# Input-projection features: the context's high and low parts in one 512-column matmul, runs of equal width, and the rotary key's high and low weights in one stationary tile

## Chip, cores and metric

The kernel runs on one core of a Trainium2 chip. The metric is the device time of one launch in microseconds (us). The core has a matrix engine (TensorE, PE in the profile; PEld is its loading of stationary tiles), a vector engine (VectorE, DVE), a scalar engine (ScalarE, ACT), GpSimd (POOL) and SyncE (SP), which here does nothing but issue DMA transfers, one after the other in program order.

## What is computed

One layer of a transformer over 512 latent tokens and 256 context tokens, width 2048, batch 1. The part that matters here is the combined input projection and the modulation that goes beside it:

```python
def _mixer_inputs(h, tabs, w_in, q_norm_w, kv_norm_w, w_uq, w_ukv):
    p = h @ w_in
    q_da = heads(p[..., :o1], DA_HEADS)
    k_da = heads(p[..., o1:o2], DA_HEADS)
    v_da = heads(p[..., o2:o3], DA_HEADS)
    c_q = _rmsnorm(p[..., o3:o4], q_norm_w)
    c_kv = _rmsnorm(p[..., o4:o5], kv_norm_w)
    k_rope = p[..., o5:][:, None]
```

`h` is the normalised and modulated input. The projection is made for the latent tokens and for the context tokens with the same weights; keys, values and the compressed key/value latent `c_kv` are wanted for both, queries and the compressed query latent `c_q` for the latent tokens alone. `k_rope`, the rotary key that all heads share, has 64 features. The keys of the latent tokens are rotated (rotary embedding). Beside it stands the conditioning, a matrix-vector product (GEMV) `silu(c) @ w_ada` of 96 blocks of 128 outputs, whose results modulate later stages. Everything is float32 to within a narrow tolerance.

## The kernel before

**Three matmuls for one product.** TensorE multiplies tiles in a reduced float32 form (`F32R`). To keep the accuracy, every operand is split into a high part (the rounded value) and a low part (what rounding left), and `mm3` makes a product out of three matmuls: high by high (L258), high by low (L259), low by high (L260). The weights arrive as blocks of 128 x 1024 float32: `wblock` (L241) has SP load the block into `wr` (L244), ACT round it into `wh` (L234), and DVE subtract to give `wl` (L235). There are three buffers each of `wr`, `wh`, `wl`.

**Stages.** Up to about 46 us a prologue normalises the input and starts the conditioning. Up to about 155 us "group 0" makes the first features of the projection beside the preparation of the 16 k-tiles of `h` (function `features(kt)`, laid out by a planner with due times, `Flow(PLAN)`). It leaves in SBUF, for each k-tile, the latent tokens' high and low parts (`hx[kt]`, two tiles `a2k` of 512 columns) and the context tokens' (`hc[kt]`, high and low, 256 columns each). Before the change, two k-tiles share a pair of `c2k` tiles: the high parts of both lie in one and the low parts of both in the other.

From about 155 to 446 us runs the part that the change is in. It is written as plain code, and the framework's scheduler sets the order of each engine's instructions; tiles are drawn from rings, and who draws a tile waits until its last reader is done.

- Seven context features, `f` = 0 to 6 in the loop: six are keys of the differential attention (`k_d[2]` to `k_d[7]`), the seventh is the rotary key (`kr_d`). Each has two weight blocks of eight k-tiles. In `feature` (L739) each k-tile makes three matmuls of 512 columns into a PSUM tile `b` (latent) and three of 256 columns into a PSUM tile `s` (context). `keys` (L685) then rotates the latent half on DVE (L304 to L307), splits both halves (L234 on ACT, L235 on DVE) into `kh` and `kl`, and `put` (L694) has SP write those to `k_d` (L696). The rotary key has 64 features; the host has laid its 64 weight columns twice beside each other in the block of 128.
- After each of these features, `next_gemv(kv, 3)` makes three GEMV blocks: SP loads 1 MB into `ada` (L323, two buffers), DVE multiplies it by the conditioning vector and sums (L326), the result is one column of `modx`. The blocks come from one list, and who calls `next_gemv` takes the next of it; the list holds 48.
- Three query-latent features, `feature(lat, None)`: latent tokens only, 48 matmuls of 512 columns each, two GEMV blocks behind each. Then `latent_norm(cq)` normalises them: its sum of squares is made by PE into a PSUM tile `s`, and DVE's `rstd` reads it last at L316 (`n`).
- The value projection, two halves of eight weight blocks, which reads `hx` and `hc` as stationary tiles 128 columns wide. Its first half takes two `s` tiles and two `b` tiles; there are only two `s` tiles, so the second of them is the one that the norm's L316 reads. Behind each weight block stand one or two GEMV blocks, until the list is empty.

Behind it the attention begins, at about 446 us, again laid out by a planner; then the output projection and the feed-forward part, to the end.

SP issues weight loads, `ada` loads and writes of keys in one order. An issue whose buffer isn't free holds up all that stand behind it.

Of the kernel before, what the change touches and what calls it, by code (L numbers as in the profile page):

```python
# [206 lines left out]
def layer_kernel(ctx: ExitStack, tc: tile.TileContext, small, rope, c_row, cc_row, x_t, ctx_t, ada, ada_k,  # L207
# [23 lines left out]
    def split(dst_h, dst_l, src, scale=None):  # L231
# [337 lines left out]
    def features(kt):  # L569
# [13 lines left out]
        for i, (src, cut, c, hl, g) in enumerate(((at_x[kt], slice(0, T), slice(0, T), xh, 1.0),  # L583
                                                  (at_c[kt // 2], o, slice(T, TT), mine, 0.6))):
            b, th = (modx, modc)[i][:, kt:kt + 1], buf(lambda: None)
            out = (slice(0, T), o)[i]
# [3 lines left out]
            step("ACT", 0.63 * g, t - 3.2 + 1.2 * i, lambda h=h, c=c, b=b, hl=hl, out=out: sc.activation(  # L590
                hl[0]()[:, out], h()[:, c], AF.Identity, bias=b), r=[th, at_b[i][kt]], w=[hl[0]])
            step("DVE", 0.67 * g, t - 2.4 + 1.2 * i, lambda h=h, c=c, b=b, hl=hl, out=out: ve.scalar_tensor_tensor(
                out=hl[1]()[:, out], in0=h()[:, c], scalar=b, in1=hl[0]()[:, out].bitcast(F32), op0=ALU.add,
                op1=ALU.subtract), r=[th, hl[0], at_b[i][kt], h], w=[hl[1]])
# [11 lines left out]
        for f in range(4):  # L606
# [4 lines left out]
            step("PE", 0.36, t + 1 + 0.1 * f + (5 if kt == KT - 1 and f > 1 else 0), mm, r=[hi, lo, *mine],  # L611
                 w=[ctx_bufs[f // 2]])

    hc_bufs = []
# [22 lines left out]
    with tc.manual_schedule(engines={mybir.EngineType.PE, mybir.EngineType.Activation, mybir.EngineType.DVE,  # L637
# [10 lines left out]
    wsrc = iter([w_f[f, hf] for f in feats for hf in range(2)] + [w_v[half, kb] for half in range(2) for kb in range(8)]  # L648
                + [w_f[7 + h, hf] for h in range(7) for hf in range(2)])
    wready = []  # L650

    def ahead(count):
        while len(wready) < count:
            src = next(wsrc, None)
            if src is None:
                return
            wready.append(wblock(src))
# [24 lines left out]
    def rtmp():  # L682
        return kv.tile([P, T], F32, tag="rt", name=nm("rt"), bufs=2)

# [1355 lines left out]
```

## Time and profile before

| | before |
|---|---|
| device time, median of 3 runs | 2364.34 us (2362.61 to 2366.74) |
| profiled execution, span from first to last instruction | 2365.8 us |
| mean granted TensorE clock | 0.992 of full speed |
| prologue and group 0, 0 to 155.6 us: PE busy | 129.8 us |
| context and query-latent features, 155.6 to 314 us: PE busy | 154.6 of 158.4 us |
| the same: DVE busy, ACT busy | 128.2 us, 38.0 us |
| the same: DMA | busy share 0.87, 313 GB/s |
| value projection, 314 to 446 us: PE busy | 132.0 of 132.0 us |
| the rest, 446 to 2365 us: PE busy | 1891.4 of 1919 us |

The span is that of one profiled execution; it lies 1.5 us above the median of the timed runs and inside their spread. Rows of the timeline give the start of an instruction in us from the span's start, its duration, engine, line and operation, output and inputs, and in brackets how long the engine stood idle before it and what ended that. Rows of groups give the busy time and the mean duration in ns of the like instructions taken together, and behind the bar the idle time just before them. Rows of waits give who waited for what: us in all, how often, the longest. The rows of the DMA view give KB of a transfer and the median us from its issue to its landing.

### The profile page before, as it was taken

To read this page: it belongs to the slowest core of one execution; us is meant where nothing else is said; L and a number is where in the kernel's file an instruction comes from. 1 tells how busy PE (TensorE), PEld (TensorE's weight loads), DVE (VectorE), ACT (ScalarE), POOL (GpSimd) and SP (SyncE) were. 2 spreads that over 40 slices of the span, in tenths; PEclk is the share of its full clock that TensorE was granted. 3 is DMA by queue.
4 is the path that set the end of the run, shared out by engine and by line. 5 is a ranking of instruction groups with operands and counts; after the bars stand their busy time and mean duration, and the time that the engine had idled before them with its cause. 6 is when DMAs were issued, how large, how long until landed. Compare 5 with 4: busy or idle time off the path is not lost.

```text
span 2365.8 us, 32444 instructions
## 1 busy us (share of the span) xinstructions
PE 2307.7 (98%) x12526; PEld 1969.6 (83%) x12526; DVE 1733.4 (73%) x2248; ACT 1140.3 (48%) x1736; POOL 255.5 (11%) x290
## 2 busy tenths in 40 slices
PE   5999999999999999999999999999999999999998
PEld 3788878888788888898888888888888888888887
DVE  8997776498977766598585858585857576767767
ACT  5331221377866622365454545454545454544546
POOL 0000000100033213000101010101010101011110
PEclk8999999999999999999999999999999999999999
DMA  9968989644411187334737464646465556465573
GB/s 350 341 251 302 324 307 342 189 138 122 146 65 40 46 331 286 103 107 112 166 105 170 113 160 118 152 125 149 127 143 134 143 135 147 119 161 125 142 189 107
DMA packets 130492, 404.25 MB, mean 171 GB/s; under 512 B 14337, under 2 KB 25089, under 8 KB 119841
## 3 DMA queue, kind: packets, MB, share of 16 engines
q1 hardware_dynamic: 103858, 351.64, 44.4%
q0 software_dynamic: 25328, 49.49, 12.0%
q8 instruction: 98, 1.61, 0.3%
q10 hardware_dynamic: 1152, 1.05, 0.1%
q14 instruction: 56, 0.46, 0.1%
HBM read 332.45 MB, written 69.67 MB: 170 GB/s over the span
## 4 chain that ended last, share of the span: by engine, by line
PE 78%; issue 9%; DVE 5%; DMA 5%; ACT 2%; POOL 1%; SPq 0%; DVEq 0%; ACTq 0%; POOLq 0%
PE y L1759 11%; PE b L258 9%; PE b L259 9%; PE b L260 9%; PE z L1759 6%; PE y L1761 5%; PE s L862 4%; PE s L258 4%; PE s L259 3%; PE s L260 3%; DMA ada<-in_ada 3%; PE z L1761 3%; PE x L1759 2%; PE f L258 2%; PE f L259 1%
## 5 line engine op out<-in xcount | busy, mean ns | idle before, releaser
L1584 DVE TENSOR_TENSOR wl<-wr,wh 128x1024 fp32r<-128x1024 f32 x144 | 176.4, 1225 | 155.8 <-ACT wh L1576 155.1
L1780 POOL DMA_DIRECT2D x_d<-xs x160 | 139.7, 1001 | 1158.7 <-ACT xs L1779 1156.3
L1576 ACT CAST wh<-wr 128x1024 fp32r<-128x1024 f32 x144 | 151.0, 1049 | 230.9 <-PE b L259 119.6
L258 PE MATMUL b<-ah,wh 128*128 128x512 f32 (+1 forms) x664 | 256.8, 387 | 0.0
L259 PE MATMUL b<-al,wh 128*128 128x512 f32 (+1 forms) x664 | 256.7, 387 | 0.0
L260 PE MATMUL b<-ah,wl 128*128 128x512 f32 (+1 forms) x664 | 255.8, 385 | 0.0
L1584 DVE TENSOR_TENSOR wl<-rb,wh 128x1024 fp32r<-128x1024 f32 x123 | 150.0, 1219 | 126.9 <-ACT wh L1576 126.9
L1576 ACT CAST wh<-rb 128x1024 fp32r<-128x1024 f32 x123 | 129.3, 1051 | 184.1 <-PE b L259 116.1
L1584 DVE TENSOR_TENSOR wl<-ws,wh 128x1024 fp32r<-128x1024 f32 x123 | 150.1, 1220 | 90.0 <-ACT wh L1576 90.0
L1576 ACT CAST wh<-ws 128x1024 fp32r<-128x1024 f32 x123 | 128.1, 1042 | 131.1 <-DVE ws L1538 45.4
L326 DVE CUSTOM_DVE_ANT_0 ada<-ada,cb,smt 128x2048 f32<-128x2048 f32 x64 | 152.6, 2391 | 43.5 <-DMA ada<-in_ada 43.4
L1759 PE MATMUL y<-a2k,wh 128*128 128x512 f32 x656 | 164.0, 392 | 0.0
L234 ACT CAST wh<-wr 128x1024 fp32r<-128x1024 f32 x53 | 55.7, 1052 | 197.5 <-DMA wr<-in_w_o 48.8
L260 PEld LDWEIGHTS b<-ah,wl 128*128 128x128 f32 x664 | 124.8, 188 | 25.7
L258 PEld LDWEIGHTS b<-ah,wh 128*128 128x128 f32 x664 | 125.1, 188 | 22.9
L259 PEld LDWEIGHTS b<-al,wh 128*128 128x128 f32 x664 | 125.1, 188 | 22.0
L258 PE MATMUL b<-a2k,wh 128*128 128x512 f32 (+1 forms) x372 | 139.2, 374 | 1.9 <-DVE n L1657 1.7
L259 PE MATMUL b<-a2k,wh 128*128 128x512 f32 (+1 forms) x372 | 138.4, 372 | 0.0
L260 PE MATMUL b<-a2k,wl 128*128 128x512 f32 (+1 forms) x372 | 137.7, 370 | 0.3 <-DVE wl L235 0.3
L1759 PEld LDWEIGHTS y<-a2k,wh 128*128 128x128 f32 x656 | 118.6, 189 | 21.6
L867 ACT ACTIVATE p<-s,m 128x768 f32<-128x768 f32 x96 | 86.8, 905 | 42.4 <-DVE m L865 39.2
L1759 PE MATMUL y<-b2k,wh 128*128 128x512 f32 x410 | 106.9, 391 | 0.0
(479 smaller groups left out, 5815.4 us busy)
## 6 DMA issues: line engine op xcount, KB each, us to landing
ada<-in_ada SPq DMA_DIRECT2D x80, 1024.0 KB, 7.0
rb<-in_w_up SPq DMA_DIRECT2D x123, 512.0 KB, 4.4
wr<-in_w_dn SPq DMA_DIRECT2D x88, 512.0 KB, 4.1
x_d<-xs POOLq DMA_DIRECT2D x160, 256.0 KB, 6.0
wr<-in_w_up SPq DMA_DIRECT2D x53, 512.0 KB, 4.2
wr<-in_w_f SPq DMA_DIRECT2D x34, 512.0 KB, 7.8
adak<-in_ada_k SPq DMA_DIRECT2D x32, 512.0 KB, 6.2
wr<-in_w_o SPq DMA_DIRECT2D x32, 512.0 KB, 6.5
```

What stands on the lines that cost most here:

```text
L234: sc.copy(dst_h, src)
L258: pe.matmul(out, st[0], mv[0], start=start, stop=False, **kw)
L259: pe.matmul(out, st[0], mv[1], start=False, stop=False, **kw)
L260: pe.matmul(out, st[1], mv[0], start=False, stop=stop, **kw)
L326: ve.tensor_tensor_reduce(out=junk, in0=w, in1=vec, op0=ALU.mult, op1=ALU.add, scale=1.0, scalar=col("b_ada", j), accum_out=dst[:, j:j + 1])
L862: pe.matmul(s()[:, c0:c1], a, b[:, c0:c1], start=i == 0, stop=i == len(ms) - 1)
L867: step("ACT", 0.9, t + cost + 1.2, lambda: sc.activation(p(), s()[:, :TT], AF.Exp, bias=m(), accum_out=lcol()), r=[s, m], w=[p, l], lag=0.25)
L1576: sc.copy(t, raw[:, k * n_:k * n_ + n_])
L1584: ve.tensor_tensor(t, raw[:, k * n_:k * n_ + n_], hi[k].bitcast(F32), op=ALU.subtract)
L1759: pe.matmul(o, w[j][0], hs[j], start=start and j == 0, stop=False, skip_group_check=True)
L1761: pe.matmul(o[:, h0], w[j][1], hs[j][:, h0], start=False, stop=j == 7, skip_group_check=True)
L1780: gp.dma_start(x1_d[dt], x, accum_op=ALU.add)
```

## The change

**The context's two parts in one matmul.** Each k-tile of the context now has a `c2k` tile of its own with the high part in columns 0 to 255 and the low part in columns 256 to 511 (`hcb[kt]` is the whole tile, `hc[kt]` the two halves). In `feature`, high weights by high context and high weights by low context become one matmul of 512 columns (`wide`) into a PSUM tile of 512 columns; low weights by high context stays a matmul of 256 columns (`narrow`) into its left half. `halves_sum` then adds the two halves: ACT copies the left one to SBUF, DVE adds the right one.

**Runs of equal width.** A weight block's matmuls are no longer ordered k-tile by k-tile but in runs: the first block's 24 latent ones, then 8 wide, then 8 narrow; the second block's 8 narrow, 8 wide, 24 latent.

**The rotary key.** Its block of 128 columns now holds the high parts of the 64 weights in columns 0 to 63 of each k-tile and the low parts in columns 64 to 127 (`rotary_block`). So a k-tile has three matmuls of 512 columns (latent high, latent low, and the context tile with both parts), and the results for high and low weights stand in the upper and lower 64 partitions; `parts_sum` adds each half to the other, so that both hold the sum, as before. The product of the two low parts is now part of the sum.

**One GEMV block** less behind the rotary key (2 instead of 3). The list is the same, so the value projection takes one more.

```diff
+    def rotary_block(src):
+        raw = wp.tile([P, 1024], F32, tag="wr", name=nm("wr"), bufs=3)
+        nc.sync.dma_start(raw, src)
+        w = wp.tile([P, 1024], F32R, tag="wh", name=nm("wh"), bufs=3)
+        sc.copy(w, raw)
+        low, src = (t.rearrange("p (k f) -> p k f", f=P)[:, :, 64:] for t in (w, raw))
+        ve.tensor_tensor(low, src, low.bitcast(F32), op=ALU.subtract)
+        return w, None
...
-        if kt % 2 == 0:
-            hc_bufs.append([buf(lambda: c2k(F32R), "c2k", 17) for _ in range(2)])
-            mine = hc_bufs[-1]
-        else:
-            mine = [buf(lambda b=b: b()) for b in hc_bufs[-1]]
+        mine = buf(lambda: c2k(F32R), "c2k", 17)
...
-                    hc[kt] = tuple(b()[:, o] for b in mine)
+                    hc[kt] = mine()[:, :C], mine()[:, C:]
+                    hcb[kt] = mine()
...
-            wready.append(wblock(src))
+            wready.append(rotary_block(src) if rotary else wblock(src))
...
+    def halves_sum(co):
+        t = kv.tile([P, C], F32, tag="ct", name=nm("ct"), bufs=2)
+        sc.copy(t, co[:, :C])
+        ve.tensor_tensor(t, co[:, C:], t, op=ALU.add)
+        return t
...
-    def feature(lat, ctxo):
+    def feature(lat, co):
         for hf in range(2):
             wh, wl = next_block()
+            ws = [(hf * 8 + j, wh[:, j * P:(j + 1) * P], wl[:, j * P:(j + 1) * P]) for j in range(8)]
+            def latent():
+                for kt, *w in ws:
+                    mm3(lat, w, hx[kt], kt == 0, kt == KT - 1)
+            def wide():
+                for kt, w, _ in ws:
+                    pe.matmul(co, w, hcb[kt], start=kt == 0, stop=False, skip_group_check=True)
+            def narrow():
+                for kt, _, w in ws:
+                    pe.matmul(co[:, :C], w, hc[kt][0], start=False, stop=kt == KT - 1, skip_group_check=True)
+            for part in (latent, wide, narrow)[::-1 if hf else 1] if co is not None else (latent,):
+                part()
+        ahead(2)
+
+    def rotary_feature(lat, co):
+        for hf in range(2):
+            w, _ = next_block()
             for j in range(8):
                 kt = hf * 8 + j
-                w = (wh[:, j * P:(j + 1) * P], wl[:, j * P:(j + 1) * P])
-                mm3(lat, w, hx[kt], kt == 0, kt == KT - 1)
-                if ctxo is not None:
-                    mm3(ctxo, w, hc[kt], kt == 0, kt == KT - 1)
+                for out, mv in ((lat, hx[kt][0]), (lat, hx[kt][1]), (co, hcb[kt])):
+                    pe.matmul(out, w[:, j * P:(j + 1) * P], mv, start=kt == 0 and mv is not hx[kt][1],
+                              stop=kt == KT - 1 and mv is not hx[kt][0])
         ahead(2)
+    def parts_sum(src, t):
+        sc.copy(t[lo], src[hi])
+        sc.copy(t[hi], src[lo])
+        ve.tensor_tensor(t, src, t, op=ALU.add)
+        return t
...
     for f in range(7):
-        lat, co = b_tile(), s_tile()
-        feature(lat, co[:, :C])
-        keys(k_d[f + 2] if f < 6 else kr_d, lat, co[:, :C])
-        next_gemv(kv, 3)
+        lat, co = b_tile(), s_tile()[:, :T]
+        if f < 6:
+            feature(lat, co)
+            keys(k_d[f + 2], lat, halves_sum(co))
+        else:
+            rotary_feature(lat, co)
+            lat = parts_sum(lat, kv.tile([P, T], F32, tag="qs0", name=nm("lt"), bufs=1))
+            keys(kr_d, lat, parts_sum(halves_sum(co), kv.tile([P, C], F32, tag="ct", name=nm("ct"), bufs=2)))
+        next_gemv(kv, 3 if f < 6 else 2)
```

The change moves instructions on four engines; all stands within the features, from about 155 us to the start of the value projection. In the rows below, the line comes first, then the operation, output and inputs with a running number of the tile, and the shape. Lines from L241 on stand 10 further down in the changed kernel, and those from `keys` on 14.

On PE, two k-tiles of a context feature before the change (`b` is the latent result, `s` the context's; `a2k` and `c2k` are the latent and context operands):

```order
L258 MATMUL b_2378<-a2k_442,wh_2345 128x512
L259 MATMUL b_2378<-a2k_455,wh_2345 128x512
L260 MATMUL b_2378<-a2k_442,wl_2346 128x512
L258 MATMUL s_2379<-c2k_449,wh_2345 128x256
L259 MATMUL s_2379<-c2k_450,wh_2345 128x256
L260 MATMUL s_2379<-c2k_449,wl_2346 128x256
L258 MATMUL b_2378<-a2k_538,wh_2345 128x512
L259 MATMUL b_2378<-a2k_566,wh_2345 128x512
L260 MATMUL b_2378<-a2k_538,wl_2346 128x512
L258 MATMUL s_2379<-c2k_568,wh_2345 128x256
L259 MATMUL s_2379<-c2k_579,wh_2345 128x256
L260 MATMUL s_2379<-c2k_568,wl_2346 128x256
```

And after it, where the first block of a context feature passes from its latent run to its wide run and then to its narrow run:

```order
L269 MATMUL b_1580<-a2k_947,wh_1472 128x512
L270 MATMUL b_1580<-a2k_849,wl_1473 128x512
L765 MATMUL s_1581<-c2k_449,wh_1472 128x512
L765 MATMUL s_1581<-c2k_472,wh_1472 128x512
L765 MATMUL s_1581<-c2k_579,wh_1472 128x512
L765 MATMUL s_1581<-c2k_568,wh_1472 128x512
L765 MATMUL s_1581<-c2k_729,wh_1472 128x512
L765 MATMUL s_1581<-c2k_764,wh_1472 128x512
L765 MATMUL s_1581<-c2k_861,wh_1472 128x512
L765 MATMUL s_1581<-c2k_956,wh_1472 128x512
L769 MATMUL s_1581<-c2k_449,wl_1473 128x256
L769 MATMUL s_1581<-c2k_472,wl_1473 128x256
```

A k-tile thus has five matmuls instead of six, and all 256-column ones of a feature stand in one run, across its two blocks. The rotary key has three per k-tile.

On SP, between the sixth key and the rotary key, before (`wr` are weight blocks, `ada` the GEMV's blocks, `kh` and `kl` the key that is written to `k_d`; the two weight blocks are those of the rotary key):

```order
L244 DMA wr_2343<-in_w_f 128x1024
L244 DMA wr_2349<-in_w_f 128x1024
L323 DMA ada_2369<-in_ada 128x2048
L696 DMA k_d_134<-kh_2228 128x768
L696 DMA k_d_134<-kl_2229 128x768
L323 DMA ada_2372<-in_ada 128x2048
L323 DMA ada_2375<-in_ada 128x2048
```

and after:

```order
L244 DMA wr_2262<-in_w_f 128x1024
L244 DMA wr_2267<-in_w_f 128x1024
L710 DMA k_d_134<-kh_2163 128x768
L333 DMA ada_2289<-in_ada 128x2048
L710 DMA k_d_134<-kl_2164 128x768
L333 DMA ada_2292<-in_ada 128x2048
L333 DMA ada_2295<-in_ada 128x2048
```

The write of `kh` has moved ahead of the first `ada` load. At two of the earlier features the third `ada` load has moved ahead of the second weight load.

On DVE, at the query-latent norm, before (`n` is L316, the last reader of the norm's `s` tile; `wl_2846` is the low part of the value projection's third weight block, the L326 rows are the GEMV):

```order
L326 ISA ada_2718,modx<-ada_2718,cb_1488,smt 128x2048
L326 ISA modx 128x1
L326 ISA ada_2721,modx<-ada_2721,cb_1488,smt 128x2048
L326 ISA modx 128x1
L235 TENSOR_TENSOR wl_2846<-wr_2843,wh_2845 128x1024
L316 TENSOR_SCALAR n_2729<-s_2724 128x512
L317 SCALAR_TENSOR_TENSOR n_2730<-nr_2728 128x512
L318 TENSOR_TENSOR n_2730<-n_2730,n_2729 128x512
```

and after:

```order
L336 ISA ada_2598,modx<-ada_2598,cb_1488,smt 128x2048
L336 ISA modx 128x1
L336 ISA ada_2601,modx<-ada_2601,cb_1488,smt 128x2048
L336 ISA modx 128x1
L326 TENSOR_SCALAR n_2609<-s_2604 128x512
L327 SCALAR_TENSOR_TENSOR n_2610<-nr_2608 128x512
L235 TENSOR_TENSOR wl_2726<-wr_2723,wh_2725 128x1024
L328 TENSOR_TENSOR n_2610<-n_2610,n_2609 128x512
```

The third value block's `wl` has moved from ahead of `n` to behind it. On PE, at the start of the value projection, the matmuls into the first `s` tile and the `b` tiles that stand ahead of the first one into the second `s` tile are 15 instead of 7. The orders of group 0, up to about 155 us, are as before on all engines.

More of the change, by code (lines that the diff above doesn't have):

```diff
@@ L609, in mm @@
                 mm3(ctx0(f), w, hc[kt], kt == 0 and f % 2 == 0, kt == KT - 1, skip=True)
-            step("PE", 0.36, t + 1 + 0.1 * f + (5 if kt == KT - 1 and f > 1 else 0), mm, r=[hi, lo, *mine],
+            step("PE", 0.36, t + 1 + 0.1 * f + (5 if kt == KT - 1 and f > 1 else 0), mm, r=[hi, lo, mine],
                  w=[ctx_bufs[f // 2]])
-    hc_bufs = []
+    hcb = [None] * KT
     g0s = [buf(s_tile, "s", 2) for _ in range(2)]
@@ L647, in layer_kernel @@
     feats = list(range(7)) + [14, 15, 16]
-    wsrc = iter([w_f[f, hf] for f in feats for hf in range(2)] + [w_v[half, kb] for half in range(2) for kb in range(8)]
-                + [w_f[7 + h, hf] for h in range(7) for hf in range(2)])
+    wsrc = iter([(w_f[f, hf], f == 6) for f in feats for hf in range(2)] + [(w_v[half, kb], False) for half in range(2) for kb in range(8)]
+                + [(w_f[7 + h, hf], False) for h in range(7) for hf in range(2)])
     wready = []
@@ L653, in ahead @@
         while len(wready) < count:
-            src = next(wsrc, None)
+            src, rotary = next(wsrc, (None, False))
             if src is None:
                 return
-            wready.append(wblock(src))
+            wready.append(rotary_block(src) if rotary else wblock(src))
     def next_block():
```

10 lines of the change are left out of this document (5 added, 5 removed).

## Prediction

> **What bounds the kernel now.** I read the page first, then the 8-us windows, the waits and the timelines of the stretch in which the changed lines run (150 to 320 us).
>
> ```profile
> span 2365.8 us, 32444 instructions
> PE 2307.7 (98%) x12526; PEld 1969.6 (83%) x12526; DVE 1733.4 (73%) x2248; ACT 1140.3 (48%) x1736; POOL 255.5 (11%) x290
> ...
> 286.00:294.00 8.00, 8.00 (x37) 6.64 (x36) 3.84 (x5) 1.05 (x1) 0.00 (x0) 1.00 0.96 372
> ...
> 302.00:310.00 8.00, 8.00 (x31) 5.37 (x29) 4.96 (x7) 2.13 (x3) 0.00 (x0) 1.00 0.84 319
> 310.00:318.00 8.00, 4.16 (x11) 3.17 (x11) 6.22 (x7) 2.26 (x3) 0.00 (x0) 0.68 0.88 327
> 318.00:326.00 8.00, 8.00 (x33) 6.52 (x32) 7.90 (x11) 2.59 (x4) 0.00 (x0) 0.89 0.71 247
> ```
>
> PE is busy 98% of the span. (Columns of a window: length, then busy time and instructions of PE, PEld, DVE, ACT, POOL, then granted clock, DMA share, GB/s.) In the changed stretch PE is full up to 310 us, then loses 3.84 of 8 us while the clock falls to 0.68. Beside it the DMA engines are 0.84 to 0.96 busy: two limits lie close together here. The wait itself, on PE:
>
> ```profile
> 309.74 0.39 PE L258 MATMUL b<-wh,c2k 128*128 128x512 f32 x1
> 313.97 0.80 PE L258 MATMUL s<-wh,a2k 128*128 128x512 f32 x1 [3.84 <-DVE n L316]
> 314.56 0.63 PE L259 MATMUL s<-wl,a2k 128*128 128x512 f32 x1
> ...
> 319.68 0.45 PE L260 MATMUL s<-wh,a2k 128*128 128x512 f32 x1
> ```
>
> This is the start of the value projection: its second `s` tile is the one that the query-latent norm has just used, and DVE's L316 (`n`) is the last to read it. What stood ahead of L316 on DVE:
>
> ```profile
> 307.09 2.35 DVE L326 CUSTOM_DVE_ANT_0 ada<-ada,cb,smt 128x2048 f32<-128x2048 f32 x1 [2.68 <-DMA ada<-in_ada]
> ...
> 309.81 2.35 DVE L326 CUSTOM_DVE_ANT_0 ada<-ada,cb,smt 128x2048 f32<-128x2048 f32 x1 [0.36 <-DMA ada<-in_ada]
> ...
> 312.09 1.22 DVE L235 TENSOR_TENSOR wl<-wr,wh 128x1024 fp32r<-128x1024 f32 x1
> 313.23 0.68 DVE L316 TENSOR_SCALAR n<-s 128x512 f32<-128x512 f32 x1
> ```
>
> So the stretch ends with DVE's queue, which waits for `ada` loads. That chain, over the whole stretch:
>
> ```profile
> L326 DVE CUSTOM_DVE_ANT_0 ada<-ada,cb,smt 128x2048 f32<-128x2048 f32 x27 | 63.4, 2348 | 21.7 <-DMA ada<-in_ada 21.7
> L235 DVE TENSOR_TENSOR wl<-wr,wh 128x1024 fp32r<-128x1024 f32 x23 | 27.9, 1218 | 2.5 <-ACT wh L234 2.4
> ...
> SPq L323 <- DVE modx L326: 75.5, 20, 7.4
> ...
> ada<-in_ada SPq DMA_DIRECT2D x26, 1024.0 KB, 7.8
> ```
>
> There are two `ada` buffers. SP issues a load when DVE has finished the buffer (SP waits 75.5 us for this), it lands after 7.8 us, DVE then takes 2.35: one `ada` per (7.8 + 2.35) / 2 = 5.1 us, whatever PE does. 27 of them stand ahead of L316.
>
> **The change part by part.** *PE work.* The period of a context feature, and matmuls without a context:
>
> ```profile
> 160.47 0.40 PE L258 MATMUL b<-a2k,wh 128*128 128x512 f32 x1
> ...
> 161.28 0.28 PE L259 MATMUL s<-c2k,wh 128*128 128x256 f32 x1
> 161.40 0.28 PE L260 MATMUL s<-c2k,wl 128*128 128x256 f32 x1
> ...
> 173.07 0.40 PE L258 MATMUL b<-a2k,wh 128*128 128x512 f32 x1
> ...
> 301.69 0.39 PE L258 MATMUL b<-a2k,wh 128*128 128x512 f32 x1
> ...
> 305.54 0.40 PE L260 MATMUL b<-a2k,wl 128*128 128x512 f32 x1
> ```
>
> From 160.47 to 173.07 lie 12 groups of three 512- and three 256-column matmuls: 1.05 us each, 16.8 us a feature. From 301.69 to 305.54 lie 17 starts of 512 columns: 0.2265 us each; a 256-column one starts 0.12 us after its like. A new feature has 48 + 16 wide and 16 narrow matmuls: 64 x 0.2265 + 16 x 0.12 = 16.4 us, 0.4 less; six give 2.3 us. The rotary one has 48 wide: 10.9 us, 5.9 less. PE work falls by 8.2 us.
>
> A rule speaks against the first part: the Trainium skill, "TensorE: Matmul & The Clock Gate", section "Part 1: The HAM clock gate", puts warm back-to-back matmuls at N / 2.4 GHz plus 2.5 ns, so one 512-column matmul in place of two of 256 would save 2.5 ns, 0.3 us over the six features (an estimate by that page). The rows differ (0.2265 and 0.12 against its 0.216 and 0.109), and the measurement decides.
>
> *What is late next.* If PE comes 8.2 us sooner to the value projection, it waits for L316 unless L316 comes sooner too. So the sum is that of L316, in four terms:
>
> - One GEMV is moved from ahead of L316 to behind it (7 x 3 + 3 x 2 = 27 become 26): one period, **-5.1**. From the bytes it would be 1.05 MB at the 319 to 372 GB/s of the windows, some 3 us.
> - L316 now stands ahead of the third value block's `wl`, not behind it: 313.23 - 312.09 = **-1.1**.
> - DVE gets seven sums of 256 columns for the context halves, and for the rotary key one of 512 and one of 256; its two low parts are half as wide.
>
> ```profile
> L307 DVE TENSOR_TENSOR rt<-rt,rt 128x512 f32<-128x512 f32 x10 | 6.8, 683 | 0.0
> ...
> L235 DVE TENSOR_TENSOR kl<-s,kh 128x256 fp32r<-128x256 f32 x7 | 2.9, 407 | 0.0
> ```
>
>  8 x 0.41 + 0.68 - 2 x (1.22 - 0.68) = 2.9 us. Bounds: 0, if they fall into the 21.7 us in which DVE waits for `ada`, and 2.9. I take **+2.9**, since in the new order they stand between two `ada` steps of a chain whose buffer is free only afterwards. The strided half-width subtraction has no row; between 0.68 (512 contiguous) and 1.22 (full width) I take 0.68, worth at most 1.1 us.
> - SP's order: the write of a key's `kh` now stands ahead of the next feature's first `ada`; before, it stood behind it. The rows of that place before:
>
> ```profile
> 245.75 0.33 SPq L323 DMA_DIRECT2D ada<-in_ada  x1
> 247.01 0.33 SPq L696 DMA_DIRECT2D k_d<-kh  x1
> 251.47 0.33 SPq L696 DMA_DIRECT2D k_d<-kl  x1
> ```
>
>  The `ada` would have gone out 1.3 us later behind `kh`. Two of the first features also have an `ada` drawn ahead of a weight load, which helps the chain. Bounds 0 and one period (5.1); I take **+2**, nearer to the 1.3 of these rows.
>
> Sum for L316: -5.1 - 1.1 + 2.9 + 2.0 = -1.3. In the new PE order 15 matmuls of the value projection run ahead of the wait, before it 7: 8 x 0.2265 = **-1.8** behind it. Together **-3.1 us**; by the bounds, -8.0 to -0.1.
>
> The first stage (up to 155 us) costs nothing: the order of all engines and the shapes are as before there. ACT's copies (seven of 256 columns, some small ones for the rotary key) hide in its idle time: ACT is 48% busy. Behind the value projection the order is as before, apart from one GEMV more, and PE runs there without a wait; a shift at its start arrives at the end.
>
> *Weights.* DVE makes the first query block's `wl` behind the third `ada` of the feature before:
>
> ```profile
> 264.11 2.34 DVE L326 CUSTOM_DVE_ANT_0 ada<-ada,cb,smt 128x2048 f32<-128x2048 f32 x1
> ...
> 266.98 1.22 DVE L235 TENSOR_TENSOR wl<-wr,wh 128x1024 fp32r<-128x1024 f32 x1
> ```
>
> It is ready at 268.2; PE needed it at 272.9 and will at 264.7, so PE waits some 3 us there, and again at the next blocks. It costs nothing as long as these waits sum to less than PE would wait for L316 anyway: 8.2 + 3.84 - 1.3 - 1.8 = 8.9 us of cover.
>
> The sum is made on the profiled span (2365.8), which lies 1.5 us above the median of the runs (2364.34) and inside their spread; I take the difference from the median: 2364.34 - 3.1 = **2361.2 us**.
>
> **The rivals.** *The waits are spread.* If the 8.9 us of waiting fall apart into pieces at the three query features and at the value projection, each shorter than the 3.84 of now, the clock may not fall: 14 matmuls from 313.97 to 319.68 took 0.41 instead of 0.2265 us, 2.5 us in all. Then -3.1 - 2.5 = -5.6: 2358.7. For it: the new `wl` waits lie in between. Against: one of them may be as long as today's. The rule that fits (the Trainium skill, same page and section): the clock halves after an idle window of about 3.4 us, and the trace agrees, with 3.84 us idle ahead of the 0.68.
>
> *PE alone sets the end.* If the DMAs land sooner, since PE no longer competes with anything of theirs, L316 comes in time: -8.2 - 3.84 - 2.5 = -14.5: 2349.8. Against: 27 periods of 5.1 us make up 138 us, just the time that the stretch takes.
>
> *The ring runs dry* (slower). More DVE work stands between `ada` steps. From the point where DVE comes to an `ada` later than it landed, the buffer is free later and each turn takes longer. DVE waited 21.7 us for `ada`, so there is room of that much, but it is uneven. If two periods are lost over the seven features, -3.1 + 10.2 = +7.1: 2371.4.
>
> *The change does less than it says*: the chain goes on as before and the moved GEMV is replaced by something else in the queue: within 1.5 us of 2364.3.
>
> **How the numbers follow.** Forecast 0.52 (own range 2356.3 to 2364.3; a quarter of it below -4.7), spread waits 0.16, PE alone 0.08, dry ring 0.14 (0.10 above +4.7), no effect 0.10. A measurement tells 0.2%, 4.7 us, from no change. Faster: 0.13 + 0.16 + 0.08 = 0.37; slower 0.10; within 0.53. The range leaves out PE alone and most of the dry ring: 2355 to 2368.
>
> **What would show it.** PE starts 0.2265 us apart in the new features and 16.4 us per feature, 10.9 for the rotary one; a wait of PE at the first query feature for `wl`; a wait for `n` at the value projection, ended at about 312.7 us; DVE's `ada` steps still some 5.1 us apart. I am wrong if L316 no longer ends a wait of PE, if the `ada` steps come closer together than 4.8 us, or if PE waits in the context features. A wait behind 460 us that was not there before would refute that the shift arrives at the end.

## The result, and the profile after

The changed kernel takes 2352.74 us (median of five runs, 2352.49 to 2354.47), the kernel before 2363.04 us (five runs, 2360.45 to 2366.74): a ratio of 0.9955, 95% interval 0.9944 to 0.9967, or 10.3 us less. The prediction was 2361.2 with a range from 2355.0: the direction was right, the size three times too small, and the time lies below the range. Four executions far from all others are left out of all medians here (3269 us of e4, 2538 of e9 and 3276 of the kernel before, each at a lower granted clock, and 4750 of e10), and since the profiles of e4 and e9 were taken in theirs, the waits of these two are not known.

The page of the changed kernel, the same two lines as before:

```profile
span 2351.0 us, 32171 instructions
PE 2299.6 (98%) x12382; PEld 1959.7 (83%) x12382; DVE 1735.9 (74%) x2257; ACT 1145.4 (49%) x1747; POOL 256.4 (11%) x290
```

Against the span of before (2365.8) that is 14.8 us, more than the 10.3 of the medians. The span is not the device time: here the same execution has 2352.74 and 2351.0, 1.7 us apart, and over all runs the two lie 1.7 to 2.2 us apart. So the profile of before was of an execution of some 2365.8 + 1.7 = 2367.5 us (an estimate), about 4.5 us above its median, and not 1.5 as "Time and profile before" and the prediction read it. In three further sets of runs the kernel before spread from 2359.2 to 2371.9 us (91 runs), and the runs of the changed kernel lay between 2352.1 and 2354.5, with one at 2359.4 (10 runs). A part of the change is that this spread has nearly gone.

The 8-us windows of the changed kernel at the place where PE stood before (length; PE, PEld, DVE, ACT, POOL; clock, DMA share, GB/s):

```profile
302.00:310.00 8.00, 8.00 (x37) 6.63 (x36) 7.75 (x9) 1.81 (x2) 0.00 (x0) 1.00 0.70 266
310.00:318.00 8.00, 8.00 (x37) 6.60 (x37) 8.00 (x9) 1.86 (x3) 0.00 (x0) 1.00 0.88 313
318.00:326.00 8.00, 8.00 (x37) 6.64 (x36) 3.60 (x5) 0.00 (x0) 0.00 (x0) 1.00 0.99 357
```

PE is full and its clock stays at 1.00. The start of the value projection, on PE:

```profile
299.86 0.79 PE L268 MATMUL s<-wh,a2k 128*128 128x512 f32 x1
...
303.70 0.39 PE L268 MATMUL s<-wh,a2k 128*128 128x512 f32 x1
```

It begins 8.1 us sooner (299.86 against 307.95). The row at 303.70 is the first into the second `s` tile, behind 15 others, and it waits for nothing. On DVE the norm's last reader, now L326, stands as follows:

```profile
295.32 2.35 DVE L336 CUSTOM_DVE_ANT_0 ada<-ada,cb,smt 128x2048 f32<-128x2048 f32 x1 [0.40 <-DMA ada<-in_ada]
...
297.74 2.35 DVE L336 CUSTOM_DVE_ANT_0 ada<-ada,cb,smt 128x2048 f32<-128x2048 f32 x1
...
301.18 0.69 DVE L326 TENSOR_SCALAR n<-s 128x512 f32<-128x512 f32 x1 [1.09 <-ACT nr L324]
```

`n` is done at 301.87, 1.8 us before PE needs the tile. It no longer waits for a GEMV block but for ACT, which follows PE's sum of squares: the chain of `ada` loads has stopped being the last one. The groups of DVE over 150 to 314 us, SP's wait for a free `ada` buffer in the same stretch, and the landing of the `ada` loads over 174 to 310 us say the same:

```profile
L336 DVE CUSTOM_DVE_ANT_0 ada<-ada,cb,smt 128x2048 f32<-128x2048 f32 x29 | 68.0, 2345 | 7.5 <-DMA ada<-in_ada 7.5
...
L696 DVE TENSOR_TENSOR ct<-s,ct 128x256 f32<-128x256 f32 x7 | 2.9, 420 | 3.0 <-ACT ct L695 3.0
...
SPq L333 <- DVE modx L336: 70.6, 18, 6.6
...
ada<-in_ada SPq DMA_DIRECT2D x28, 1024.0 KB, 6.2
```

Two more blocks are done in the same window, and DVE waits 7.5 us for them instead of 21.7. SP waits 70.6 us for a buffer instead of 75.5, and a load lands 6.2 us after its issue instead of 7.8. The added sums have the predicted duration (0.42 us).

PE's work in the new forms, from its timeline:

```profile
160.92 1.98 PE L765 MATMUL s<-c2k,wh 128*128 128x512 f32 x8
162.73 2.08 PE L769 MATMUL s<-c2k,wl 128*128 128x256 f32 x16
164.64 0.63 PE L765 MATMUL s<-c2k,wh 128*128 128x512 f32 x2
...
166.48 0.39 PE L268 MATMUL b<-a2k,wh 128*128 128x512 f32 x1
...
182.93 0.39 PE L268 MATMUL b<-a2k,wh 128*128 128x512 f32 x1
...
254.16 0.61 PE L782 MATMUL b<-a2k,wh 128*128 128x512 f32 x2
...
265.04 0.39 PE L268 MATMUL b<-a2k,wh 128*128 128x512 f32 x1
```

From one second block's latent run (166.48) to the next (182.93) is a feature: 16.45 us, where 16.4 was predicted and 16.8 it was. The rotary key takes 265.04 - 254.16 = 10.88 us (predicted 10.9). A narrow matmul costs (164.64 - 162.73) / 16 = 0.12 us.

The middle of the value projection turned out to matter. There its six PSUM tiles are split and copied out (`v`, L235 on DVE), and the second half needs them again:

```profile
359.85 2.35 DVE L336 CUSTOM_DVE_ANT_0 ada<-ada,cb,smt 128x2048 f32<-128x2048 f32 x1
...
363.69 0.69 DVE L235 TENSOR_TENSOR v<-s,v 128x512 fp32r<-128x512 f32 x1 [1.48 <-ACT v L234]
364.29 2.34 DVE L336 CUSTOM_DVE_ANT_0 ada<-ada,cb,smt 128x2048 f32<-128x2048 f32 x1
```

In the changed kernel the first `v` waits for ACT alone. Last, PE's first wait in the attention, which marks the end of the stretch, before and after:

```profile
461.23 0.50 PE L862 MATMUL s<-ks,qs 128*128 128x512 f32 x1 [0.68 <-ACT p L867]
```

```profile
446.23 0.50 PE L910 MATMUL s<-ks,qs 128*128 128x512 f32 x1 [0.68 <-ACT p L915]
```

It comes 15.0 us sooner, and the spans differ by 14.8: what lies behind it has the same length to 0.2 us.

### The profile page after: what moved, and what is told of

It is laid out like the page before. It is cut to its first block, busy times and chain, and to the rows that moved or that the text cites. A ratio compares the mean times of both kernels' runs of the same rounds, so it can differ in the third digit from the quotient of the medians.

```text
span 2351.0 us, 32171 instructions
## 1 busy us (share of the span) xinstructions
PE 2299.6 (98%) x12382; PEld 1959.7 (83%) x12382; DVE 1735.9 (74%) x2257; ACT 1145.4 (49%) x1747; POOL 256.4 (11%) x290
## 4 chain that ended last, share of the span: by engine, by line
PE 59%; issue 31%; DVE 4%; POOL 3%; ACT 2%; DMA 1%; SPq 0%; POOLq 0%; DVEq 0%; ACTq 0%
PE b L268 6%; PE b L270 6%; PE b L269 6%; PE y L1807 5%; PE s L910 4%; POOL x_d L1828 3%; PE s L268 3%; PE s L270 3%; PE s L269 3%; PE z L1807 3%; PE y L1809 3%; PE f L268 2%; PE f L269 1%; PE f L270 1%; PE pt L930 1%
## 5 line engine op out<-in xcount | busy, mean ns | idle before, releaser
L268 PE MATMUL b<-a2k,wh 128*128 128x512 f32 (+1 forms) x356 | 132.0, 371 | 1.9 <-DVE n L1705 1.6
L270 PE MATMUL b<-a2k,wl 128*128 128x512 f32 (+1 forms) x356 | 131.5, 369 | 0.4 <-DVE wl L235 0.4
L269 PE MATMUL b<-a2k,wh 128*128 128x512 f32 (+1 forms) x356 | 131.4, 369 | 0.0
```

Source lines behind the costliest of these rows:

```text
L268: pe.matmul(out, st[0], mv[0], start=start, stop=False, **kw)
L269: pe.matmul(out, st[0], mv[1], start=False, stop=False, **kw)
L270: pe.matmul(out, st[1], mv[0], start=False, stop=stop, **kw)
```

## The experiments

The theory after the result: PE's work alone sets the length of the stretch in the changed kernel; in the kernel before, loads come late at two gates, the norm's `n` at the start of the value projection and the `v` splits in its middle, because GEMV blocks stand ahead of both on DVE. The rival is the prediction's own: the GEMV's ring runs at its own pace and the moved block is what came off it.

The stretch length in the table is taken from the profile, from PE's first matmul behind the context norm (near 155.6 us) to the wait at the attention's start; blocks ahead are those of this stretch that stand ahead of `n` and of the first `v` in DVE's order. Medians are in us, with the kernel before as it was measured beside each. Listed are waits of 0.5 us and more, and any at `n`; waits for the value splits, of which one (`nr`) lies in a buffer of the norm, are put down as `v`.

| kernel | median (before beside it) | ratio, 95% interval | blocks ahead of `n` / first `v` | stretch | waits of PE in it |
|---|---|---|---|---|---|
| before | 2363.04 | | 27 / 42 | 305.6 | 3.84 `n` |
| changed | 2352.74 (2363.04) | 0.9955, 0.9944 to 0.9967 | 26 / 39 | 290.5 | none |
| e1 before again | 2363.38 (2364.37) | 0.9995, 0.9984 to 1.0005 | 27 / 42 | 303.6 | 0.35 `n`; 0.55, 1.90 `v` |
| e2 norm's own tile | 2369.79 (2364.37) | 1.0024, 1.0012 to 1.0036 | 27 / 42 | 306.1 | 4.65 at the end |
| e3 before, less PE | 2360.51 (2364.37) | 0.9983, 0.9971 to 0.9994 | 26 / 40 | 303.1 | 6.75, 1.45, 0.53 weights; 0.70, 2.08 `v` |
| e4 changed, GEMV back | 2358.24 (2364.37) | 0.9978, 0.9966 to 0.9989 | 26 / 40 | | |
| e5 the same | 2356.79 (2362.51) | 0.9970, 0.9956 to 0.9984 | 26 / 40 | 295.7 | 2.43 `v` |
| e6 before, GEMV moved | 2365.14 (2362.51) | 1.0011, 1.0000 to 1.0021 | 27 / 41 | 307.7 | 2.94 `n`; 2.80, 1.42 `v` |
| e7 rotary part alone | 2362.78 (2362.51) | 0.9993, 0.9980 to 1.0006 | 26 / 40 | 303.3 | 2.38, 1.68 weights; 2.73 `v` |
| e8 k-tile order | 2354.55 (2362.51) | 0.9965, 0.9951 to 0.9978 | 26 / 39 | 293.8 | 1.22 `n` |
| e9 changed again | 2353.12 (2362.77) | 0.9965, 0.9953 to 0.9977 | 26 / 39 | | |
| e10 context part alone | 2357.31 (2362.77) | 0.9977, 0.9968 to 0.9986 | 27 / 41 | 297.6 | 1.44 `v` |
| e11 before, 12 blocks fewer | 2360.70 (2362.77) | 0.9991, 0.9980 to 1.0002 | 27 / 36 | 298.6 | none |
| e12 changed, blocks earlier | 2359.43 (2362.77) | 0.9987, 0.9977 to 0.9996 | 26 / 40 | 296.9 | 2.45, 0.54 weights |

**e1, the kernel before again.** No edit.

> The kernel before, unchanged. In its profiled execution PE waits 3.84 us for the norm's L316 at the start of the value projection and then runs 14 matmuls slowly (2.5 us); its runs spread from 2360.5 to 2366.7 us, those of the changed kernel only from 2352.5 to 2354.5. If the wait is what differs between executions, this profile shows a wait of another length, anything from 0 to 4 us, and its span is shorter than 2365.8 by what the wait and the slow matmuls lack. If the wait is the same in every execution, it is 3.6 to 4.1 us here and the span within 1 us of 2365.8, or differs by something elsewhere.

The profile of e1 has the wait at `n` at 0.35 us, and two others where the first profile had none. On PE, and what stood ahead on DVE:

```profile
309.70 0.50 PE L258 MATMUL s<-wh,a2k 128*128 128x512 f32 x1 [0.35 <-DVE n L316]
...
383.88 0.47 PE L258 MATMUL s<-wh,c2k 128*128 128x512 f32 x1 [1.90 <-DVE nr L235]
```

```profile
369.75 2.35 DVE L326 CUSTOM_DVE_ANT_0 ada<-ada,cb,smt 128x2048 f32<-128x2048 f32 x1 [1.86 <-DMA ada<-in_ada]
...
372.57 2.35 DVE L326 CUSTOM_DVE_ANT_0 ada<-ada,cb,smt 128x2048 f32<-128x2048 f32 x1 [0.47 <-DMA ada<-in_ada]
...
374.85 0.69 DVE L235 TENSOR_TENSOR v<-s,v 128x512 fp32r<-128x512 f32 x1
...
380.17 0.69 DVE L235 TENSOR_TENSOR v<-b,n 128x512 fp32r<-128x512 f32 x1 [2.31 <-DMA v_d<-v]
380.78 2.34 DVE L326 CUSTOM_DVE_ANT_0 ada<-ada,cb,smt 128x2048 f32<-128x2048 f32 x1
...
383.05 0.69 DVE L235 TENSOR_TENSOR nr<-s,nq 128x512 fp32r<-128x512 f32 x1
```

So the wait that carried the whole prediction differs from execution to execution, between 0.35 and 3.84 us here; where PE doesn't wait at `n`, it comes to the middle sooner and waits there: 0.55 us behind a `v` with two blocks ahead of it whose loads are late, then 1.90 us for the split `nr`, which stands behind a write of `v` to memory and one more block.

**e2, the norm in a tile of its own.** The kernel before, with

```diff
     def latent_norm(tiles, squares, width, dim, wname, dst):
-        s = s_tile()
+        s = s_tile() if width == TT else b_tile()
```

> The kernel before, with the query-latent norm's sum of squares in one of the four b tiles instead of one of the two s tiles, so that the value projection's second s tile no longer waits for L316. DVE's order is the same. If the wait was worth 3.84 + 2.5 us and nothing else is late behind it, the profiled span is 2359 to 2360.5 and the median 1 to 5 us below the kernel before (2363.0). If something else ends the wait in its place, the value projection starts no sooner and the time is within 1 us of the kernel before.

Neither case of the expectation came: the wait at `n` is gone, and the kernel is 5.4 us slower than before.

```profile
442.38 0.80 PE L258 MATMUL f<-a2k,wh 128*128 128x512 f32 x1 [4.65 <-DVE v L235]
```

The attention's first `f` tile now waits for a `v` split at the end of the value projection, where no other kernel here has a wait. That the `b` ring has moved on by one tile would explain it; it wasn't tried apart. The run says that removing one wait of this stretch can bring in a larger one at the next gate, but it doesn't size the gate at `n`.

**e3, less work for PE.** The kernel before, with

```diff
                 if ctxo is not None:
-                    mm3(ctxo, w, hc[kt], kt == 0, kt == KT - 1)
+                    pe.matmul(ctxo, w[0], hc[kt][0], start=kt == 0, stop=False)
+                    pe.matmul(ctxo, w[1], hc[kt][0], start=False, stop=kt == KT - 1)
```

> The kernel before, with the context's matmul of high weights by low inputs left out of the seven context features: 112 matmuls of 0.12 us, 13.4 us of PE work less; DMAs, ACT and DVE work as before. If the GEMV's ring paces itself (5.1 us per block, as the prediction had it), its 26th block still ends near 309 us in the profile, PE reaches the value projection near 294 us and waits some 11 us there: time 2358 to 2363. If the ring follows PE through SP's order of issue, the 26th block ends near 297 us, PE waits less than 2 us, and the time is 2345 to 2350.

PE has 13.4 us less to do (this kernel leaves out a part of the product), and the time falls by 3.9. The time lies in the range of the expectation's first case, but not for its reason. The 26th block ends at 309.3 us: the ring did not follow PE, as the prediction had it, but PE's wait is not at `n`:

```profile
269.57 0.79 PE L258 MATMUL b<-a2k,wh 128*128 128x512 f32 x1 [6.75 <-ACT wh L234]
```

That is the first query feature's first block. SP issues its load at 258.0 us, behind the write of the last key and three `ada` loads, and ACT has it at 268.5; PE came to it at 262.8. In the changed kernel the same load goes out at 253.1 and PE comes to it at 265.0. PE work that is taken away turns into waits wherever a load is next.

**e4 and e5, the GEMV block put back** into the changed kernel:

```diff
-        next_gemv(kv, 3 if f < 6 else 2)
+        next_gemv(kv, 3)
```

> The changed kernel with three GEMV blocks behind the rotary key again, as before. If the moved block was worth a period of the ring (5.1 us), L316 comes 5 us later than in the changed kernel, PE waits about 4 us at the start of the value projection, and the time is 4 to 6 us above 2352.7. If the scheduler places L316 by itself and the ring follows PE, the time is within 1 us of 2352.7.

> The changed kernel with three GEMV blocks behind the rotary key again; its nine undisturbed runs lay at 2355.1 to 2362.8 us, some 6 us above the changed kernel's 2352.7, and this is a look at where. SP's order now has an ada load ahead of the two weight blocks of the first query feature. If that load is what is late, PE waits 3 to 7 us for wh or wl near 265 us, and not for L326 at the value projection. If the ring with one block more is what is late, PE waits for L326 near 302 us, by 3 to 5 us.

The medians are 2358.24 and 2356.79, 5.5 and 4.1 us above the changed kernel; by the gains over the kernel before, each measured beside its own (6.1 and 5.7 here, 10.3 and, in e9, 9.7 there), the block is worth 3.5 to 4.6. That is near the 5.1 that it was priced at. The place is another than predicted, though, and another than either case of e5's expectation. The scheduler puts 26 blocks ahead of `n` in this kernel too, and PE doesn't wait there or at the first query feature; it waits in the middle of the value projection, where 40 blocks stand ahead instead of 39:

```profile
370.69 0.47 PE L268 MATMUL s<-wh,a2k 128*128 128x512 f32 x1 [2.43 <-DVE v L235]
```

**e6, the GEMV block moved in the kernel before,** the reverse: `next_gemv(kv, 3 if f < 6 else 2)` and nothing else.

> The kernel before with only the GEMV block moved (2 instead of 3 behind the rotary key). PE's work is as before, so if the place of the loads alone made the gain, the time is some 6 us below the kernel before, near 2358. If the moved block is worth something only where PE's work is shorter (PE reaches the loads before they land), it is within 2 us of the kernel before.

2365.14 against 2362.51: no gain, at most a small loss. 27 blocks are still ahead of `n`. The moved block is worth its 3.5 to 4.6 us only together with the shorter PE work. The profile was of the longest run (2370.61), with three waits:

```profile
313.43 0.79 PE L258 MATMUL s<-wh,a2k 128*128 128x512 f32 x1 [2.94 <-DVE n L316]
...
382.34 0.47 PE L258 MATMUL s<-wh,a2k 128*128 128x512 f32 x1 [2.80 <-DVE v L235]
386.50 0.47 PE L258 MATMUL s<-wh,c2k 128*128 128x512 f32 x1 [1.42 <-DVE nr L235]
```

**e7, the rotary part alone.** The changed kernel with the old `feature` and `keys(k_d[f + 2], lat, co[:, :C])`, three GEMV blocks.

> The changed kernel with the six context keys in the old form (three matmuls of 256 columns, k-tile by k-tile) and three GEMV blocks behind the rotary key: the rotary part alone. PE's work is 5.9 us less than before. If PE's work is what counts, the time falls by 5 to 6 us (2358). If the loads in SP's queue are what counts, PE waits for the first query feature's weights, for L326 or in the value projection, and the time falls by 0 to 3 us (2361 to 2364).

5.9 us less PE work, and 2362.78 against 2362.51: nothing. Its profile has 6.8 us of waits:

```profile
280.33 0.50 PE L268 MATMUL b<-a2k,wh 128*128 128x512 f32 x1 [2.38 <-ACT wh L234]
282.75 0.77 PE L270 MATMUL b<-a2k,wl 128*128 128x512 f32 x1 [1.68 <-DVE wl L235]
...
377.97 0.47 PE L268 MATMUL s<-wh,a2k 128*128 128x512 f32 x1 [2.73 <-DVE v L235]
```

**e8, k-tile by k-tile** instead of runs of equal width:

```diff
-            for part in (latent, wide, narrow)[::-1 if hf else 1] if co is not None else (latent,):
-                part()
+            for kt, *w in ws:
+                mm3(lat, w, hx[kt], kt == 0, kt == KT - 1)
+                if co is not None:
+                    pe.matmul(co, w[0], hcb[kt], start=kt == 0, stop=False, skip_group_check=True)
+                    pe.matmul(co[:, :C], w[1], hc[kt][0], start=False, stop=kt == KT - 1, skip_group_check=True)
```

> The changed kernel with the matmuls of a context feature k-tile by k-tile (three latent, one wide, one narrow) instead of in runs of equal width. If mixing widths costs what it did before the change (1.05 us for a k-tile where its pieces alone make 1.04), a feature takes 16.5 to 16.7 us instead of 16.45 and PE's work rises by 0.5 to 1.5 us. The scheduler's order of loads differs too: with the ada loads placed as well as in the changed kernel the time is 2353 to 2355; if not, waits of PE add 3 to 7 us, near 2358.

2354.55, some 1.5 to 2 us above the changed kernel. A feature takes 16.66 us, by the rows of two successive ones:

```profile
181.97 0.39 PE L268 MATMUL b<-a2k,wh 128*128 128x512 f32 x1
```

```profile
198.63 0.39 PE L268 MATMUL b<-a2k,wh 128*128 128x512 f32 x1
```

So of the 0.35 us that a feature gained, 0.14 come from joining two matmuls into one, and 0.21 from the runs. That it is the widths, and not the change of output tile, fits the rotary key: its matmuls alternate between `b` and `s` too, all 512 columns wide, and 48 of them take 10.88 us, 0.2267 each, as without a change of tile. The 0.21 is 1.3 us over six features, and the profile has a wait of 1.22 us at `n` besides. The scheduler's order of loads differs from the changed kernel's at the first features, with 26 and 39 blocks ahead as there, and there is no wait in the middle.

**e9, the changed kernel again.** No edit.

> The changed kernel, unchanged, beside the others of this call. If PE alone sets its time in this stretch, its runs lie close together again (2352 to 2356), its profile shows no wait of PE over 0.5 us between 156 and 445 us, and the value projection's first half is copied out (DVE, first v) near 364 us with 39 GEMV blocks of this stretch ahead of it. If it only happened to have no wait in the one profile, a wait of 1 to 4 us stands at L326 or at the middle of the value projection, and the runs spread over 6 us or more.

Five runs at 2352.1, 2352.5, 2353.1, 2354.2 and 2359.4: close together, except that one of ten runs by now is some 6 us longer, for a reason that no profile shows. That PE has no wait in the changed kernel thus rests on one profile.

**e10, the context part alone.** The changed kernel with every weight block from `wblock`, `feature` for all seven, and `next_gemv(kv, 3)`.

> The context part alone: all seven context features with the wide matmul and runs of equal width, the rotary key with split weights as before, three GEMV blocks behind it. PE's work is some 2.5 us less than before; 27 GEMV blocks stand ahead of the norm's L326 and 41 ahead of the first v. If PE's work is what counts, the time falls by 2 to 3 us. If the GEMV blocks ahead of these two places are what counts, it is within 2 us of the kernel before, with PE waiting 1 to 4 us at the middle of the value projection or its start.

2357.31, 5.5 us below the kernel before beside it, twice its PE work (2.5 us: seven features by 0.35): both cases missed. Its stretch is 297.6 us, and one wait is left:

```profile
375.07 0.47 PE L268 MATMUL s<-wh,a2k 128*128 128x512 f32 x1 [1.44 <-DVE v L235]
```

With this part the loads come sooner although 27 and 41 blocks stand ahead: the 26th block ends at 302.2 us, against 309.4 in the first profile of the kernel before and 305.5, 303.9 and 304.5 in those of e1, e2 and e11, which have its order up to there. The loads themselves land sooner: over 174 to 310 us, the window of the prediction's row, the median `ada` load lands after 5.8 us here and after 6.2, 6.1 and 5.9 in the other kernels with runs of equal width (changed, e5, e12), against 6.7 to 7.8 in all the others (before, e1, e2, e3, e6, e7, e8, e11). Why is not settled. The order of SP differs at the first features, and at one of them the key's write.

**e11, twelve GEMV blocks fewer** in the kernel before:

```diff
-    gv = iter([64 + i for i in range(16)] + [48 + i for i in range(16)] + [32 + i for i in range(16)])
+    ve.memset(modx[:, 36:48], 0.0)
+    gv = iter([64 + i for i in range(16)] + [48 + i for i in range(16)] + [32 + i for i in range(4)])
```

> The kernel before, with the last 12 of the 48 GEMV blocks of this stretch left out (12 MB less to load; their results are set to zero). 27 blocks still stand ahead of L316, but 36 instead of 42 ahead of the value projection's first v. If the loads behind PE are what makes the kernel before slower than its PE work, the waits at the middle of the value projection vanish; only the one at its start may stay, and the median falls by 1 to 4 us, with the fastest runs where those of before are (2359.2). If PE alone sets the time of the kernel before, it is within 1 us of it.

2360.70 against 2362.77, with four of ten runs at 2359.5 to 2359.8, where the fastest of the kernel before lie; the interval reaches to 1.0002, so the median's fall is not clear by itself. The profile, of the shortest run, has no wait of PE over 0.4 us in the stretch, at whose end stands:

```profile
454.06 0.50 PE L863 MATMUL s<-ks,qs 128*128 128x512 f32 x1 [0.68 <-ACT p L868]
```

This is an execution of the kernel before without late loads: 298.6 us of stretch, against 290.5 in the changed kernel. PE has no wait over 0.4 us in either and its granted clock is 1.00 throughout in both, so the difference, 8.1 us, is PE's work, predicted at 8.2. That PE doesn't wait at `n` here is a draw: the same 27 blocks stand ahead of `n` as before.

**e12, GEMV blocks earlier** in the changed kernel:

```diff
-            next_gemv(kv, 1 if (half * 8 + kb) % 3 else 2)
+            next_gemv(kv, 2 if not half else 1)
```

> The changed kernel with two GEMV blocks behind every weight block of the value projection's first half, so that 40 instead of 39 stand ahead of its first v and 42 instead of 40 or 41 ahead of the later ones; the list of 48 is the same and ends sooner. If these blocks are what makes the wait, PE waits 2 to 5 us at the middle of the value projection, with the slow clock behind it, and the time is 2355 to 2359. If the wait is a matter of PE's work alone, it is 2352 to 2354.

2359.43, just above the 2355 to 2359 of the first case: the loads alone, with PE's work unchanged, cost 6 us against e9. The waits lie in the middle, a little later than expected, and for weights that stand behind the blocks rather than for `v`:

```profile
385.53 0.73 PE L268 MATMUL b<-wh,a2k 128*128 128x512 f32 x2 [2.45 <-ACT wh L234]
386.80 0.80 PE L269 MATMUL b<-wl,a2k 128*128 128x512 f32 x1 [0.54 <-DVE wl L235]
```

## Why the prediction was wrong

**What came is a rival with a chance of 0.08,** "PE alone sets the end". Its -14.5 us was the difference of the two profiles (14.8), and its terms hold for these two: 8.1 of PE work, the 3.84 us wait, and the slow clock behind it. Its time, 2349.8, was still 2.9 us below the measured one, because it was set off against the median; from the 2367.5 us of the profiled execution it would be 2353.0. The direction of the forecast came out right in part by luck: its largest gain, the moved block's 5.1 us at L316, did not fall there, and PE's 8.2 us, which it held to be hidden, did come.

**PE's work: right.** 8.2 us predicted, 8.1 by e11 against the changed kernel, with 0.35 a feature and 5.9 at the rotary key (8.0 together). By the Trainium skill (TensorE: Matmul & The Clock Gate, Part 1: The HAM clock gate) joined matmuls would have given an estimated 0.24 us over the six features (96 pairs at 2.5 ns; the prediction has 0.3). The measurement decides: e8 shows 0.14 us a feature, 0.8 in all, from joining alone, and the runs of equal width gave more than that.

**The step that failed: "the sum is that of L316".** Its end was put 1.3 us sooner; it came 12 us sooner in the profile, where `n` begins at 301.2, and some 7.7 us sooner than in e1 and e11 (309.0 and 308.9). Three things were wrong in it.

- The base. 313.23 us was the latest `n` of the four profiles with that order (e2 has 307.68). A wait that depends on when loads land was taken from one execution, and the span was set against a device time without the 1.7 us between them.
- The pace, "one `ada` per 5.1 us, whatever PE does". In the changed kernel the first 26 blocks took, from the end of the first to the end of the last, 123.0 us, or 4.92 a turn; in the kernel before 5.31 and 5.18 (e1). That is above the 4.8 that the prediction had named as a sign of being wrong, but over 25 turns it is 6.4 to 9.9 us less. The formula took the landing of a load, 7.8 us, as fixed; it was 6.7 in e1 and 6.2 in the changed kernel. With these it gives 4.5 and 4.3 us a turn, less than was measured, so the two buffers alone do not set the pace. The two costs that I put on it, +2.9 for the sums and +2.0 for SP's order, were not measured apart; the turns became shorter in spite of them. Half of the clause holds: in e3 the ring did not run faster for 13.4 us less of PE.
- The moved block, -5.1 at L316. `n` stands behind 26 blocks without the move too (e4, e5), and behind 27 with it in the kernel before (e6). The scheduler puts 27 there in the kernels with PE's old work or 2.5 us less of it, and 26 where PE has 5.9 us or more less, so it appears to go by its own estimate of PE's time, which wasn't tried. The block's 3.5 to 4.6 us fell due at another gate.

**"A shift at its start arrives at the end": the second gate was missed.** The start is that of the value projection. It did arrive in the changed kernel, but not of itself: the middle of the value projection was taken for open because the first profile has no wait there; it had none because PE was already late by the wait at `n`. 42 blocks stood ahead of the first `v` before, 39 after. Had the loads not moved too, PE's 8.1 us could have been lost there in part, as 2.73 us and the slow clock behind them were in e7.

**The wait for weights at the first query feature** (some 3 us) did not come: DVE began that `wl` at 262.62 and had it ready at 263.84, 1.6 us before PE used it. The same 18 blocks stand ahead of it as before, but the eighteenth began at 259.74 instead of 264.11 (262.22 in e1). So the ring was ahead by this place already, before the moved block could count, and e5, without the move, has that `wl` at 262.30.

**Where the 10.3 us come from.** By e9 and e11, measured side by side (9.7 us in all): 2360.70 - 2353.12 = 7.6, put down to PE's work, and 2362.77 - 2360.70 = 2.1, put down to loads that were late in some executions of the kernel before and no longer are. The second number rests on e11, whose interval touches no change. The parts do not add: rotary alone 0, context alone 5.5, both 5.7 to 6.1 (e5 and e4 against the kernel before beside them), both with the moved block 10.

**What stays open.** Why the context part brings the blocks in sooner (e10), and why the rotary part alone doesn't. By one profile of each kernel the shorter landing goes with the runs of equal width and not with the joined matmul, which e8 has too (7.0 us); whether PE's order does it or the order of SP that comes with it, no run separates. It would take the same instructions in two orders of SP to tell, which the scheduler doesn't offer and which wasn't tried.

## What to carry to other kernels

Where PE and the loads are both near their limit, work taken off PE is worth only what the next load allows: list every place where PE waits for something that stands behind loads, not only the one that shows a wait, since an early wait hides the later ones. A wait that ends with a DMA is a draw from a spread; look at a second execution, or at the range of the runs, before its length is made a term of a sum. And where a scheduler sets the order, an edit of the source moves an instruction only if the scheduler's clock agrees; read the place from the order, and don't credit it to the line that was edited.

## What the runs showed of the hardware

The granted clock does not follow the length of a wait alone. After 2.43 us of waiting in e5 it fell to 0.58 in the next four microseconds, in e1 after 1.90 us to 0.57, and in e6 it stayed at 1.00 through a wait of 2.80 us and one of 1.42 (windows; the clock is the first number behind the engines' columns, ahead of DMA share and GB/s):

```profile
368.00:372.00 4.00, 1.57 (x8) 1.12 (x7) 3.09 (x6) 2.02 (x3) 0.00 (x0) 1.00 0.97 331
372.00:376.00 4.00, 4.00 (x12) 3.14 (x11) 4.00 (x6) 1.17 (x2) 0.00 (x0) 0.58 1.01 303
```

```profile
378.00:382.00 4.00, 1.53 (x7) 0.94 (x5) 3.35 (x4) 1.12 (x3) 0.00 (x0) 1.00 0.90 314
382.00:386.00 4.00, 2.74 (x11) 1.99 (x11) 3.40 (x5) 1.88 (x3) 0.00 (x0) 1.00 0.84 255
386.00:390.00 4.00, 3.50 (x15) 2.93 (x16) 2.77 (x4) 0.59 (x1) 0.00 (x0) 1.00 1.13 340
```

The prediction cited 3.4 us from the Trainium skill (TensorE: Matmul & The Clock Gate, Part 1: The HAM clock gate) as the length of an idle window that halves the clock. It is not a threshold for a single wait: the traces of e5 and e1 have a drop after waits shorter than that, and e6 has none after a wait longer than theirs. Mixing 512- and 256-column matmuls cost 0.21 us over a feature's 80 matmuls (16.66 against 16.45 us), though each width in a run of its own keeps a steady rate (0.2267 and 0.12 us).
